# Split weights at sixteen different distances modulo 256 bytes from the activations, in a two-layer decoder kernel

## The chip, the cores and the metric

One core of a Trainium2 chip. The time is the device time of one execution in microseconds (us). Three runs of the kernel before gave a median of 1256.75 us (1255.97 to 1258.51).

## What is computed

Two layers over 256 positions of 1024 channels in float32: `x += 0.5*post1(SwiGLU_1(pre1(x)))`, then `x += postm(MIX(prem(x)))`, then a second SwiGLU step. MIX is one input projection that feeds three causal mixers (A: gated MLP over chunks of 128, B: dilated attention, C: stick-breaking attention), a sigmoid-gated merge and an output projection.

```
h = rms_norm(x, ffn1_pre_g[l])
x = x + 0.5 * rms_norm(swiglu(h, ffn1_wi[l], ffn1_wo[l]), ffn1_post_g[l])
h = rms_norm(x, mix_pre_g[l])
y = hybrid_mixer(h, w_in[l], ...)          # branches A, B, C, gates, w_o
x = x + rms_norm(y, mix_post_g[l])
h = rms_norm(x, ffn2_pre_g[l])
x = x + 0.5 * rms_norm(swiglu(h, ffn2_wi[l], ffn2_wo[l]), ffn2_post_g[l])
```

In branch C the scores get a strictly causal mask (0 or -1e30) before the log-space sums.

## The kernel before

**Weights.** All weights come as 1 MB units of 128 x 2048 float32, by SyncE's DMA queue, into two `raw` buffers (or, for some units of the FFNs that are combined by addition, into other tiles). The coroutine `splitter` (line 213) cuts each half unit into a high and a low part in the type fp32r: ScalarE writes `hi` (line 231), VectorE writes `lo = raw - hi` (line 232). Both go into a ring of eight buffers each, `hi` and `lo`, 128 x 1024 elements or 4096 bytes a partition (lines 228 and 229; the few units in `place` go to other tiles of the same size). A ring buffer comes free when the last matmul on it has been issued (`release`, line 266).

**Matmuls.** Activations are split in the same way into `hT`, `gT`, `yT` and `sA` tiles. `mm3` (line 391) adds three products: activation high times weight high (line 392), activation high times weight low (393), activation low times weight high (394). So of each three matmuls two stream a `hi` buffer and one a `lo` buffer; the 128 x 128 activation block is the stationary operand (a weight load, PEld, of its own before each matmul), the split weights are the moving operand, 512 columns at a time (256 in line 715). In `qk` (lines 670 to 699) the roles are exchanged: ring buffers are stationary, `hT` moves.

**Addresses.** The pools lie one behind another, `cp` (constants, `x`, `hT`), `rp` (`raw`, `hi`, `lo`) and `sp` (all else); within a pool tiles follow in the order in which their tags are first used, each in slots of a multiple of 32 bytes. After the 4-byte tile `mh` (line 273) every tile of `cp` and `rp` is a multiple of 256 bytes long, and in `sp` the small statistics tiles fill eight slots of 32 bytes. So `hT`, `raw`, all `hi` and `lo`, `gT`, `yT` and `sA` start at the same address modulo 256. Slices taken of them start at multiples of 512 bytes. Only `ident`, ahead of `mh`, starts 32 bytes lower modulo 256; it is the moving operand of the transposes (line 339), whose stationary operand is a tile of `sp`. In line 650 (branch A's gating, plain float32, two passes a matmul) `ws` is stationary and `v` moves: both at the common address modulo 256.

**Masks.** `load_consts` (line 298) runs once, in the first FFN. It loads two parts of the constants into tiles of the tag `w3` (four buffers, which also serve the FFN's `sg` and `cc` tiles) and casts them with VectorE into `mB` (bf16) and `uo`; the third part goes by DMA straight into `mC` (float32), which line 821 adds to branch C's scores, 16 times.

**Order.** A planner of estimated costs (`Clock`, the numbers after `yield`) sets the order in which coroutines issue their instructions; each engine takes its own in that order.

Of the kernel before, what the change touches and what calls it, by code (L numbers as in the profile page):

```python
# [9 lines left out]
F32 = mybir.dt.float32  # L10
F32R = mybir.dt.float32r
BF16 = mybir.dt.bfloat16
# [3 lines left out]
P = 128  # L16
# [19 lines left out]
def f32(ap):  # L36
    return ap.bitcast(F32)
# [40 lines left out]
def trunk(ctx, tc, x, wpk, gains, lnp, wst, bst, consts, out, depth=DEPTH):  # L78
    nc = tc.nc
    V, S, G, T = nc.vector, nc.scalar, nc.gpsimd, nc.tensor  # L80
    ck = Clock()

    cp = ctx.enter_context(tc.tile_pool(name="cp", bufs=1))
    rp = ctx.enter_context(tc.tile_pool(name="rp", bufs=2))
# [7 lines left out]
    def nm(s):  # L92
        cnt[0] += 1
        return f"{s}_{cnt[0]}"
# [7 lines left out]
    def w3_tile(n):  # L102
        return sp.tile([P, 768], F32, tag="w3", name=nm(n), bufs=4)
# [3 lines left out]
    RING = 8  # L107
    raws, halves, place = {}, {}, {}
    st_ = {"dma": 0, "pos": 0, "ring": 0, "free": RING}
# [3 lines left out]
    def load(dst, src):  # L113

        i = nc.sync.dma_start(dst, src)
        if lastdma[0] is not None:
            tc.add_manual_dep(i.ins, lastdma[0].ins.name, NOSYNC, reason="load order")
        lastdma[0] = i
# [9 lines left out]
    for l in range(depth):  # L128
        for st0, qj in ((0, QUADS), (33, None), (73, QUADS)):
            b = UNITS * l + st0  # L130
# [77 lines left out]
    def ready(n, kind, k):  # L208
        if kind[0] == "T":
            raw[n] = k.b if kind == "T3" else k.ffn["a" if kind == "T1" else "f"]  # L210
        return n in raw

    def splitter():
        for n, (kind, k) in enumerate(plan):
            while not ready(n, kind, k):
                next(ld)
            halves[n] = []
            for q in range(2):
                gate = place.get(n)
                while st_["free"] <= 0 if gate is None else not gate.on:  # L220
                    yield 0.2
                    gate = place.get(n)
                if gate is not None:
                    h = sp.tile([P, 1024], F32R, tag="q4", name=f"hi{n}_{q}", bufs=9)
                    lo = sp.tile([P, 1024], F32R, tag="q4", name=f"lo{n}_{q}", bufs=9)
                else:
                    st_["free"] -= 1
                    h = rp.tile([P, 1024], F32R, tag="hi", name=f"hi{n}_{q}", bufs=RING)
                    lo = rp.tile([P, 1024], F32R, tag="lo", name=f"lo{n}_{q}", bufs=RING)
                r = raw[n][q]  # L230
                S.copy(h, r)  # L231
                V.tensor_sub(lo, r, f32(h))  # L232
                halves[n].append((h, lo))
                yield 1.2
            if kind == "B11":
                f = k.ffn
                if "f" not in f:
                    f["f"] = [sp.tile([P, 1024], F32, tag="xn", name=nm("wf"), bufs=2) for _ in WQ]
                for q, c in enumerate(WQ):
                    V.tensor_add(f["f"][q], f["a"][q], k.b[q])  # L240
                    nc.gpsimd.dma_start(f["a"][q], wpk[k.u12][:, c], accum_op=ALU.add)
                    yield 0.6
            elif kind == "B21":
                for q in range(2):
                    V.tensor_add(k.ffn["f"][q], k.ffn["f"][q], raw[n][q])
                    yield 0.6
            elif kind == "T1":
                k.t1 = True
            done.add(n)
            for _ in range(3):  # L250
                next(ld, None)
# [41 lines left out]
    mB = [mB_[:, 768:1152], mB_[:, 0:768]]  # L293
    uo = cp.tile([P, 256], F32R, tag="uo", name="uo")
    nU, nO = uo[:, 0:P], uo[:, P:256]
    mC = cp.tile([P, 384], F32, tag="mC", name="mC")

    def load_consts():
        a = w3_tile("cst")
        load(a, consts[:, 0:768])  # L300
        V.tensor_copy(mB_[:, 0:768], a)
        a = w3_tile("cst")
        load(a[:, 0:640], consts[:, 768:1408])
        V.tensor_copy(mB_[:, 768:1152], a[:, 0:384])
        V.tensor_copy(uo, a[:, 384:640])
        load(mC, consts[:, 1408:1792])

    hT = cp.tile([P, NT, KD, 2, P], F32R, tag="hT", name="hT")
    hh, hl = hT[:, :, :, 0, :], hT[:, :, :, 1, :]
# [124 lines left out]
    def ffn(gi, nxt, first):  # L434
# [149 lines left out]
        for j in range(2, NCH - 1):  # L584
            if j == 4:
                if first:
                    load_consts()
                gain(gi + 1)
                gain(gi + 2)
            if j // 2 * 2 in QUADS:  # L590
                if j % 2 == 0:
                    pair7(j, ss)
                continue
            uo = take(1)[0]
            wo(uo, j - 2, 0, False)
            wo(uo, j - 2, 1, True)
            us = take(2)
            wi(us, j, 0, False)
            wi(us, j, 1, True)
# [335 lines left out]


    ck.start(splitter(), 7.0)
    for tt in range(NT):
        hready[tt] = Flag()
# [5 lines left out]
    for l in range(depth):  # L945
        b = 6 * l
# [102 lines left out]
```

## Time and profile before

| | |
|---|---|
| median of the runs | 1256.75 us |
| profiled execution, time / span | 1256.99 / 1255.3 us |
| TensorE matmuls | 1237.2 us, 99% of the span |
| weight loads | 1013.0 us, beside the matmuls |
| VectorE / ScalarE | 958.0 us (76%) / 738.7 us (59%) |
| DMA | 259.38 MB, 207 GB/s |

The span runs from the first instruction to the last; 1.7 us lie around it. A busy TensorE is not TensorE at its peak: matmuls overlap and their ends are modelled, so the pace of matmuls is read from the distance between their starts. Line numbers are those of the kernel before.

### The profile page before, as it was taken

The page shows a single profiled execution, that of the slowest core. Times are in us where ns is not written, and L with a number is a line of the kernel's source. Part 1 is how long each engine was busy: PE and PEld are TensorE (multiplying, and loading weights), DVE is VectorE, ACT ScalarE, POOL GpSimd, SP SyncE. Part 2 cuts the span into 40 slices and gives each one's busy share as a digit, 9 for nine tenths or more (in the row PEclk, how much of TensorE's full clock was granted, in tenths as well). Part 3 has the DMA queues.
Part 4 walks back from the last instruction along what each step waited for, and adds up shares of the span by engine and source line. Part 5 has one row for each costly group of instructions (what it writes and reads, how often), then busy time and mean ns, then how long its engine had stood idle before and what let it go on. Part 6 is the DMA issues. An engine that isn't in the chain of part 4 may idle for free.

```text
span 1255.3 us, 15804 instructions
## 1 busy us (share of the span) xinstructions
PE 1237.2 (99%) x5964; PEld 1013.0 (81%) x5964; DVE 958.0 (76%) x1215; ACT 738.7 (59%) x1026; POOL 77.2 (6%) x129
## 2 busy tenths in 40 slices
PE   8999999999999999999999999999999999999997
PEld 6777888888778888888888888888877788788886
DVE  5789977746765878899768899866477668688983
ACT  5566655545666465666645676654466655556662
POOL 0001001000000010010011000010000000111000
PEclk8999999999999999999999999999999999999999
DMA  7899555554335557895668785645543355687851
GB/s 252 273 320 268 173 201 193 191 212 173 129 135 183 188 181 268 253 284 170 248 215 244 257 256 194 238 167 182 188 170 132 134 201 201 202 240 241 255 186 66
DMA packets 45293, 259.38 MB, mean 207 GB/s; under 512 B 5280, under 2 KB 5408, under 8 KB 21280
## 3 DMA queue, kind: packets, MB, share of 16 engines
q1 hardware_dynamic: 38304, 233.20, 51.4%
q0 software_dynamic: 6912, 25.17, 10.6%
q8 instruction: 47, 0.77, 0.2%
q14 instruction: 30, 0.25, 0.1%
HBM read 257.30 MB, written 1.05 MB: 206 GB/s over the span
## 4 chain that ended last, share of the span: by engine, by line
PE 83%; DVE 6%; DMA 5%; ACT 3%; issue 1%; POOL 1%; SPq 0%; DVEq 0%; POOLq 0%; ACTq 0%
PE mm L392 15%; PE mm L394 15%; PE mm L393 15%; PE qk L681 6%; PE acc L394 5%; PE acc L393 5%; PE acc L392 5%; DMA raw<-wpk 4%; DVE lo L232 4%; PE qk L685 3%; PE tr L339 2%; ACT hi L231 2%; PE pj L392 1%; PE pj L394 1%; PE pj L393 1%; PE wo L394 1%
## 5 line engine op out<-in xcount | busy, mean ns | idle before, releaser
L232 DVE TENSOR_TENSOR lo<-raw,hi 128x1024 fp32r<-128x1024 f32 x376 | 453.0, 1221 | 121.1 <-ACT hi L231 115.9
L231 ACT CAST hi<-raw 128x1024 fp32r<-128x1024 f32 x376 | 387.5, 1050 | 191.6 <-DMA raw<-wpk 73.9
L392 PE MATMUL mm<-hi,hT 128*128 128x512 f32 x784 | 314.4, 401 | 1.5 <-ACT hT L332 1.5
L394 PE MATMUL mm<-hi,hT 128*128 128x512 f32 x784 | 307.7, 392 | 0.2 <-DVE hT L333 0.2
L393 PE MATMUL mm<-lo,hT 128*128 128x512 f32 x784 | 307.2, 392 | 0.0
L392 PEld LDWEIGHTS mm<-hi,hT 128*128 128x128 f32 x784 | 148.0, 189 | 33.1 <-issue 2.7
L394 PEld LDWEIGHTS mm<-hi,hT 128*128 128x128 f32 x784 | 147.8, 188 | 32.6 <-DVE hT L333 0.9
L393 PEld LDWEIGHTS mm<-lo,hT 128*128 128x128 f32 x784 | 148.2, 189 | 28.0
L392 PE MATMUL acc<-hi,gT 128*128 128x512 f32 x352 | 139.4, 396 | 0.0
L393 PE MATMUL acc<-lo,gT 128*128 128x512 f32 x352 | 137.9, 392 | 0.0
L394 PE MATMUL acc<-hi,gT 128*128 128x512 f32 x352 | 137.8, 392 | 0.0
L681 PE MATMUL qk<-hT,hi 128*128 128x512 f32 x320 | 111.3, 399 | 0.0
L685 PE MATMUL qk<-hT,lo 128*128 128x256 f32 x320 | 83.4, 281 | 0.0
L392 PE MATMUL mm<-hi,sA 128*128 128x512 f32 x192 | 77.2, 402 | 0.6 <-DVE sg L479 0.6
L394 PEld LDWEIGHTS acc<-hi,gT 128*128 128x128 f32 x352 | 66.2, 188 | 13.9 <-DVE gT L333 0.3
L393 PEld LDWEIGHTS acc<-lo,gT 128*128 128x128 f32 x352 | 66.2, 188 | 13.0
L392 PEld LDWEIGHTS acc<-hi,gT 128*128 128x128 f32 x352 | 66.2, 188 | 12.8
L394 PE MATMUL mm<-hi,sA 128*128 128x512 f32 x192 | 75.2, 392 | 0.0
L393 PE MATMUL mm<-lo,sA 128*128 128x512 f32 x192 | 75.0, 390 | 0.0
L332 ACT CAST gT<-tr 128x256 fp32r<-128x256 f32 x88 | 32.5, 369 | 64.2 <-PE tr L339 63.8
L681 PEld LDWEIGHTS qk<-hT,hi 128*128 128x128 f32 x320 | 57.8, 189 | 10.5
L685 PEld LDWEIGHTS qk<-hT,lo 128*128 128x128 f32 x320 | 60.5, 189 | 3.6
(168 smaller groups left out, 1623.7 us busy)
## 6 DMA issues: line engine op xcount, KB each, us to landing
raw<-wpk SPq DMA_DIRECT2D x187, 1024.0 KB, 4.8
wb<-wpk SPq DMA_DIRECT2D x24, 512.0 KB, 6.9
wb<-wpk POOLq DMA_DIRECT2D x24, 512.0 KB, 8.6
wa<-wpk SPq DMA_DIRECT2D x24, 512.0 KB, 6.0
wa<-wpk POOLq DMA_DIRECT2D x24, 512.0 KB, 9.2
gain<-gains SPq DMA_DIRECT2D x12, 512.0 KB, 7.5
x<-x SPq DMA_DIRECT2D x2, 512.0 KB, 5.6
raw<-wpk SPq DMA_DIRECT2D x2, 512.0 KB, 6.3
```

What stands on the lines that cost most here:

```text
L231: S.copy(h, r)
L232: V.tensor_sub(lo, r, f32(h))
L332: lasthi[0] = S.copy(h_out, src)
L339: T.transpose(tr[:, k * P:(k + 1) * P], src[:, k * P:(k + 1) * P], ident)
L392: T.matmul(o, ah, bh, start=first, stop=False, skip_group_check=go_on)
L393: T.matmul(o, ah, bl, start=False, stop=False, skip_group_check=go_on)
L394: T.matmul(o, al, bh, start=False, stop=stop, skip_group_check=go_on)
L681: T.matmul(o, h, hT[:, :, k, :, :], start=k == 0, stop=k == KD - 1)
L685: T.matmul(o[:, :, 0, :], lo, hh[:, :, k, :], start=False, stop=False)
```

## The change

A new helper `ring_half` gives each of the 16 ring buffers a tag of its own and a length of 1032 elements (4128 bytes), of which 1024 are used from element `b` on. With 32 bytes more a buffer, the pool lays `hi0`, `lo0`, `hi1`, `lo1` and so on 32 bytes apart modulo 256; `b` adds up to 28 bytes. The starts of the used parts lie, modulo 256 bytes from the activations: `hi` 0 to 7 at 0, 64, 128, 192, 4, 72, 144, 216; `lo` 0 to 7 at 32, 100, 168, 236, 48, 116, 184, 252. The ring still has eight pairs and each buffer is used again after eight. `mC` becomes bf16 (768 bytes a partition less, against 512 more for the ring): its constants are loaded into a third `w3` tile, and VectorE casts them.

```
--- before.py
+++ after.py
@@ -210,6 +210,13 @@
             raw[n] = k.b if kind == "T3" else k.ffn["a" if kind == "T1" else "f"]
         return n in raw
 
+    def ring_half(kind, n, q):
+
+        i = st_["ring"] % RING
+        t = rp.tile([P, 1032], F32R, tag=f"{kind}{i}", name=f"{kind}{'ABCDEFGH'[i]}_{n}_{q}", bufs=1)
+        b = i if kind == "lo" else (0, 0, 0, 0, 1, 2, 4, 6)[i]
+        return t[:, b:b + 1024]
+
     def splitter():
         for n, (kind, k) in enumerate(plan):
             while not ready(n, kind, k):
@@ -225,8 +232,8 @@
                     lo = sp.tile([P, 1024], F32R, tag="q4", name=f"lo{n}_{q}", bufs=9)
                 else:
                     st_["free"] -= 1
-                    h = rp.tile([P, 1024], F32R, tag="hi", name=f"hi{n}_{q}", bufs=RING)
-                    lo = rp.tile([P, 1024], F32R, tag="lo", name=f"lo{n}_{q}", bufs=RING)
+                    h, lo = ring_half("hi", n, q), ring_half("lo", n, q)
+                    st_["ring"] += 1
                 r = raw[n][q]
                 S.copy(h, r)
                 V.tensor_sub(lo, r, f32(h))
@@ -293,7 +300,7 @@
     mB = [mB_[:, 768:1152], mB_[:, 0:768]]
     uo = cp.tile([P, 256], F32R, tag="uo", name="uo")
     nU, nO = uo[:, 0:P], uo[:, P:256]
-    mC = cp.tile([P, 384], F32, tag="mC", name="mC")
+    mC = cp.tile([P, 384], BF16, tag="mC", name="mC")
 
     def load_consts():
         a = w3_tile("cst")
@@ -303,7 +310,9 @@
         load(a[:, 0:640], consts[:, 768:1408])
         V.tensor_copy(mB_[:, 768:1152], a[:, 0:384])
         V.tensor_copy(uo, a[:, 384:640])
-        load(mC, consts[:, 1408:1792])
+        a = w3_tile("cst")
+        load(a[:, 0:384], consts[:, 1408:1792])
+        V.tensor_copy(mC, a[:, 0:384])
 
     hT = cp.tile([P, NT, KD, 2, P], F32R, tag="hT", name="hT")
     hh, hl = hT[:, :, :, 0, :], hT[:, :, :, 1, :]
```

## Rows read from the trace of the kernel before

**Rows 1.** The profile's page, part 1: busy time, share of the span, instructions.

```profile
PE 1237.2 (99%) x5964; PEld 1013.0 (81%) x5964; DVE 958.0 (76%) x1215; ACT 738.7 (59%) x1026; POOL 77.2 (6%) x129
```

**Rows 2.** The page, part 4: the chain that ended last, by engine.

```profile
PE 83%; DVE 6%; DMA 5%; ACT 3%; issue 1%; POOL 1%; SPq 0%; DVEq 0%; POOLq 0%; ACTq 0%
```

**Rows 3.** All waits of TensorE, longest first: who for whom, us in total, times, longest.

```profile
PE tr L339 <- DVE sg L452: 3.9, 5, 1.7
```

**Rows 4.** Groups by line and shape, TensorE: busy us, mean ns | idle before.

```profile
L392 PE MATMUL mm<-hi,hT 128*128 128x512 f32 x784 | 314.4, 401 | 1.5 <-ACT hT L332 1.5
...
L392 PE MATMUL wo<-hi,hT 128*128 128x512 f32 x64 | 25.5, 399 | 0.0
```

**Rows 5.** Timeline of TensorE, 512 columns: start us, us, engine, line, instruction.

```profile
600.01 0.39 PE L394 MATMUL mm<-hi,hT 128*128 128x512 f32 x1
...
604.77 0.39 PE L394 MATMUL mm<-hi,hT 128*128 128x512 f32 x1
```

**Rows 6.** Timeline of TensorE, 256 columns (line 715).

```profile
268.59 0.28 PE L393 MATMUL mmv<-lo,hT 128*128 128x256 f32 x1
...
270.39 0.28 PE L393 MATMUL mmv<-lo,hT 128*128 128x256 f32 x1
```

**Rows 7.** One line's instructions: duration ns min/median/max; weight loads of 64, 128, 128 columns.

```profile
L855 PEld LDWEIGHTS avC<-eC,vC x32: 137/137/138, 332.8 to 999.2; 128*64 128x64 f32 x32
L392 PEld LDWEIGHTS mm<-hi,hT x784: 186/188/334, 10.5 to 1239.2; 128*128 128x128 f32 x196
L650 PEld LDWEIGHTS sv<-v,ws x32: 187/192/193, 221.4 to 847.5; 128*128 128x128 f32 x32
```

**Rows 8.** The same view, the matmuls of lines 650 and 339.

```profile
L650 PE MATMUL sv<-v,ws x32: 270/275/276, 221.5 to 847.6; 128*128 128x128 f32 x32
L339 PE MATMUL tr<-ident,mg x32: 270/272/273, 426.7 to 1050.8; 128*128 128x128 f32 x32
```

**Rows 9.** Timeline of TensorE: eight matmuls of line 650, four transposes of line 339.

```profile
221.54 1.05 PE L650 MATMUL sv<-v,ws 128*128 128x128 f32 x8
...
426.67 0.60 PE L339 MATMUL tr<-ident,mg 128*128 128x128 f32 x4
```

**Rows 10.** Timeline of TensorE in `qk`: moving operand in two runs.

```profile
280.08 0.28 PE L685 MATMUL qk<-hT,lo 128*128 128x256 f32 x1
...
281.84 0.28 PE L685 MATMUL qk<-hT,lo 128*128 128x256 f32 x1
```

**Rows 11.** Timeline of TensorE in branch C: 256 columns in two runs.

```profile
328.12 0.28 PE L839 MATMUL cu<-sh,uo 128*128 128x256 f32 x1
...
328.48 0.29 PE L842 MATMUL cu<-sh,uo 128*128 128x256 f32 x1
```

**Rows 12.** Groups by line and shape, VectorE: two operands in SBUF.

```profile
L232 DVE TENSOR_TENSOR lo<-raw,hi 128x1024 fp32r<-128x1024 f32 x376 | 453.0, 1221 | 121.1 <-ACT hi L231 115.9
...
L491 DVE TENSOR_TENSOR sA<-hT 128x512 f32<-128x512 f32 x16 | 10.8, 684 | 0.0
```

**Rows 13.** The same view: branch C's mask, branch B's bf16 mask, the cast to bf16.

```profile
L821 DVE TENSOR_TENSOR zC<-z,mC 128x384 f32<-128x384 f32 x16 | 8.3, 553 | 4.6 <-PE z L814 4.6
...
L738 DVE CUSTOM_DVE_ANT_0 pB<-s0B,mB 128x384 f32<-128x384 f32 x8 | 4.4, 550 | 0.0
...
L304 DVE CAST mB<-cst 128x384 bf16<-128x384 f32 x1 | 0.4, 360 | 0.3 <-DMA cst<-consts 0.3
```

**Rows 14.** Timelines of SyncE, VectorE, TensorE around the constants, with `mC`'s landing time.

```profile
74.74 0.44 SPq L115 DMA_DIRECT2D mC<-consts  x1
...
DMA to landing us min/median/max: 9.4/9.4/9.4
...
83.90 0.29 DVE L305 CAST uo<-cst 128x256 fp32r<-128x256 f32 x1
...
91.18 0.50 PE L392 MATMUL mm<-hi,sA 128*128 128x512 f32 x1 [0.56 <-DVE sg L479]
```

More of the change, by code (lines that the diff above doesn't have):

```diff
@@ L211, in ready, with ring_half @@
         return n in raw
+    def ring_half(kind, n, q):
+        i = st_["ring"] % RING
+        t = rp.tile([P, 1032], F32R, tag=f"{kind}{i}", name=f"{kind}{'ABCDEFGH'[i]}_{n}_{q}", bufs=1)
+        b = i if kind == "lo" else (0, 0, 0, 0, 1, 2, 4, 6)[i]
+        return t[:, b:b + 1024]
     def splitter():
@@ L227, in splitter @@
                     st_["free"] -= 1
-                    h = rp.tile([P, 1024], F32R, tag="hi", name=f"hi{n}_{q}", bufs=RING)
-                    lo = rp.tile([P, 1024], F32R, tag="lo", name=f"lo{n}_{q}", bufs=RING)
+                    h, lo = ring_half("hi", n, q), ring_half("lo", n, q)
+                    st_["ring"] += 1
                 r = raw[n][q]
@@ L295, in trunk @@
     nU, nO = uo[:, 0:P], uo[:, P:256]
-    mC = cp.tile([P, 384], F32, tag="mC", name="mC")
+    mC = cp.tile([P, 384], BF16, tag="mC", name="mC")
     def load_consts():
@@ L305, in load_consts @@
         V.tensor_copy(uo, a[:, 384:640])
-        load(mC, consts[:, 1408:1792])
+        a = w3_tile("cst")
+        load(a[:, 0:384], consts[:, 1408:1792])
+        V.tensor_copy(mC, a[:, 0:384])
     hT = cp.tile([P, NT, KD, 2, P], F32R, tag="hT", name="hT")
```

## The prediction

> **What bounds the kernel.** I read the busy times of the page first: matmuls fill 99% of the span, VectorE 76%, ScalarE 59% [rows 1]. The chain of work that ended last agrees: 83% of it is TensorE [rows 2]. Then the waits of TensorE: the largest of all comes to 3.9 us in the whole run [rows 3]. So the time is the pace of matmuls, and the next thing to read is the distance between their starts.
>
> In the timeline, 21 steps of matmuls with 512 columns take 604.77 - 600.01 = 4.76 us, 226.7 ns each [rows 5]. Fifteen steps with 256 columns take 270.39 - 268.59 = 1.80 us, 120 ns each [rows 6]. The difference, 106.7 ns for 256 columns, is 0.417 ns a column; 512 columns are 213.3 ns. Each matmul, long or short, so pays 13.3 ns on top. As it doesn't grow with the columns, it belongs to the change of weights, one load for each matmul. The groups of 512 columns on lines 392 to 394 run from `hT` with 784 for each line to `wo` with 64 for each [rows 4]; with the three groups between them (352, 192 and 80 for each line) that is 3 x 1472 = 4416 matmuls, 4416 x 13.3 ns = 58.7 us. This is what the change can act on: its moving operands, and what is loaded while they stream, now start at the same address modulo 256.
>
> **Part 1: the distances.** The question is whether the 13.3 ns come from both reads meeting at equal addresses modulo 256. A weight load of 64 columns takes 137 ns, one of 128 columns 188 ns [rows 7]: 0.80 ns a column, about twice the time of a moving column (0.417). While a load reads its 512 bytes (128 x 0.80 = 102 ns), the moving side reads 102 / 0.417 = 245 columns, 980 bytes. The distance between the two reads doesn't stay at its start: it grows by some 470 bytes, nearly two turns of 256. Whatever the start, the reads pass each other about equally often. A start of 0 isn't a lasting state, and another start takes nothing away.
>
> There is also a place where both go at one pace. On line 650 a load takes 192 ns, like the slow ones [rows 7], and the matmul's 128 columns take (1050 - 275) / 7 = 110.7 ns [rows 8, 9], also about 0.83 ns a column; the distance 0 is held from end to end. If equal addresses cost, it would be here. It pays 110.7 - 106.7 = 4.0 ns above 256 times 0.417 ns. The transposes, at distance 32, take (600 - 272) / 3 = 109.3 ns [rows 8, 9], 2.6 ns above. So distance 0, held throughout, costs at most 4.0 ns, and 1.4 ns more than distance 32; the 13.3 ns appear where it isn't held. (These are float32 matmuls, not fp32r, so it is a neighbour and no proof.) I take the gain of the distances as zero, with 0 and 13.3 ns as the ends.
>
> The trace shows 13.3 ns with each load. [...]
>
> **Part 2: odd starts.** The new starts are 4 to 28 bytes off the 32-byte grid for `hi` 4 to 7 and for `lo` 1 to 7. Per turn of the ring a `hi` is used twice and a `lo` once: 4 x 2 + 7 = 15 of 24 uses, 15/24 x 4416 = 2760 matmuls. No moving operand of the trace starts so; it may break its rows once more than now. The nearest rows are moving operands in two runs. In branch C three steps of 256 columns in two runs take 328.48 - 328.12 = 0.36 us, 120 ns [rows 11]: no more than in one run. In `qk`, five pairs (512 and 256 columns, two runs each) take 281.84 - 280.08 = 1.76 us, 352 ns a pair [rows 10], against 226.7 + 120 = 346.7: 2.7 ns a matmul. Ends: 0 and 2760 x 2.7 ns = 7.4 us. I take 0, because branch C's matmuls stream split data past a constant block as `mm3` does, while `qk` has its roles exchanged. A gain below nothing is excluded by no row and stands with the first rival.
>
> On VectorE, the split of 1024 elements takes 1221 ns and an addition of 512 takes 684 ns [rows 12]: (1221 - 684) / 512 = 1.05 ns an element, and the constant part is 147 ns. I cost odd starts at nothing here. What covers it is VectorE's quarter of idle time; were 100 ns added to each of the 376 splits of [rows 12], it would be 38 us on an engine with 1255.3 - 958 = 297 us to spare, and only in the stretches where TensorE waits for a split would any of it show.
>
> **Part 3: the mask.** Removed: nothing. Added: one DMA target that is a `w3` tile, and one cast of 128 x 384 to bf16, 0.36 us [rows 13]. Branch C's addition reads bf16 in place of float32: 16 x 553 ns before, and branch B's operation of the same width with a bf16 mask takes 550 ns [rows 13], so no change. The cast waits for its DMA: issued at 74.74, landed 9.4 us later at 84.14; the cast before it in VectorE's order ends at 83.90 + 0.29 = 84.19 [rows 14], so the wait is near zero. Queued behind it on VectorE are the splits, and TensorE waited 0.56 us for VectorE at 91.18 [rows 14], so VectorE is last there and 0.4 us goes on the path (0 if a later DMA hides it, 0.8 if the landing slips). SyncE's queue has the gains and the next `raw` unit behind the third load; a `w3` buffer last used two tiles earlier is free by then, so I cost that at nothing. If it weren't, SyncE would hold those loads until the transposes of the FFN's last `sg` tile are done.
>
> **Sum.** Distances 0, odd starts 0, mask +0.4 us. The profiled execution took 1256.99 us for a span of 1255.3; its sum is 1257.4. The median of the runs lies 0.24 us under the profiled one: 1257.2 us.
>
> **Rivals.**
> 1. *The distance matters in full.* For: the 13.3 ns are the same in all places, and all of them have distance 0. Against: the drift of nearly two turns and line 650. Only `hi` 0 stays at 0, 2 uses of 24: 4416 x 22/24 = 4048 matmuls x 13.3 ns = 53.8 us, 1203 us. If only half the distances help, some 1230.
> 2. *It matters as on lines 650 and 339.* 1.4 to 4.0 ns a matmul, say 2.7: 4048 x 2.7 = 10.9 us, 1246 us.
> 3. *Odd starts cost (the other side).* The place is the moving read of the 2760 matmuls, the price up to 2.7 ns [rows 10]: up to 7.4 us, 1265 us; at 2 ns, 1263. It decides from 1 ns a matmul (2.8 us). For: no large operand now starts off the 32-byte grid. Against: branch C's two runs at no price. [...]
> 4. *Odd starts cost much*: the affected streams fall to half their pace, 213 ns more. With the five buffers that start at odd multiples of 4 bytes (`hi` 4, `lo` 1, 3, 5, 7; 6 uses of 24): 1104 x 213 ns = 235 us, 1492 us. Nothing in the trace speaks for it.
> 5. *The change doesn't do what it says*: should the pool lay out the tiles in another order, the starts are other ones, and with them the cases above; the distances of 0 and the 32-byte shifts keep it among them. It has no chance of its own.
>
> **How the numbers follow.** Forecast 0.49, rival 1 0.14, rival 2 0.14, rival 3 0.18, rival 4 0.05. What a measurement of this kernel can tell from no change is about 0.2%, 2.5 us, so the forecast counts as no change, rivals 1 and 2 as faster, 3 and 4 as slower: 0.28, 0.49, 0.23. The range reaches from rival 2 to rival 3, 1245 to 1265 us (0.81). The forecast's own range is 1255 to 1259.
>
> **What would show each step.** The distance between starts of 512-column matmuls: 226.7 ns for all 16 buffers if I am right; 213 to 224 for some or all by rivals 1 and 2; by rival 3, higher on the buffers with odd starts alone, and it would then sort by `b`. Line 650 and the transposes, whose operands don't move, must keep 110.7 and 109.3 ns. VectorE's split stays at 1221 ns, line 821 at 553 ns. A third cast of 0.36 us stands near 84 us, with TensorE's wait near 91 us longer by about as much. The prediction is wrong if the 13.3 ns change by more than 0.5 ns on the mean.

## The result, and the profile after

| | before | after |
|---|---|---|
| median of the runs | 1256.36 us | 1270.99 us |
| ratio, 95% interval | | 1.0111 [1.0092, 1.0131] |
| profiled execution, time / span | 1256.99 / 1255.3 us | 1268.84 / 1267.1 us |

The changed kernel is 1.1% slower, outside the predicted range (1245 to 1265 us). The medians are from runs taken side by side; 1256.36 us is the same kernel as the 1256.75 us above. The profiled execution of the changed kernel is the shortest of its four. TensorE's granted clock is 0.996 in both profiled executions.

The page of the changed kernel, part 1 (busy us, share of the span, instructions) and the first line of part 4 (the chain that ended last, by engine):

```profile
PE 1253.0 (99%) x5964; PEld 1015.6 (80%) x5964; DVE 960.9 (76%) x1216; ACT 738.5 (58%) x1026; POOL 77.5 (6%) x129
...
PE 95%; DVE 2%; DMA 1%; ACT 1%; POOL 0%; issue 0%; SPq 0%; DVEq 0%; POOLq 0%; ACTq 0%
```

Matmuls are busy for 15.8 us more than in [rows 1], with as many instructions; VectorE and ScalarE have changed by 2.9 and 0.2 us. On the chain TensorE's share rose from 83% [rows 2] to 95%: TensorE takes longer, and waits less for the others. So the pace of matmuls comes next. The timeline of TensorE (start us, us, engine, line, instruction) in a stretch of 48 steps of 512 columns which both kernels run through without a break; first the kernel before:

```profile
545.56 0.48 PE L392 MATMUL mm<-hi,sA 128*128 128x512 f32 x1
545.87 0.39 PE L393 MATMUL mm<-lo,sA 128*128 128x512 f32 x1
546.11 0.40 PE L394 MATMUL mm<-hi,sA 128*128 128x512 f32 x1
546.34 0.39 PE L392 MATMUL mm<-hi,sA 128*128 128x512 f32 x1
...
547.49 0.39 PE L394 MATMUL mm<-hi,sA 128*128 128x512 f32 x1
547.71 0.39 PE L392 MATMUL acc<-hi,gT 128*128 128x512 f32 x1
547.94 0.39 PE L393 MATMUL acc<-lo,gT 128*128 128x512 f32 x1
...
556.55 0.39 PE L392 MATMUL mm<-hi,sA 128*128 128x512 f32 x1
556.78 0.39 PE L393 MATMUL mm<-lo,sA 128*128 128x512 f32 x1
```

The kernel after, the same work (its lines 401 to 403 are lines 392 to 394 of before):

```profile
549.40 0.47 PE L401 MATMUL mm<-hiE,sA 128*128 128x512 f32 x1
549.71 0.39 PE L402 MATMUL mm<-loE,sA 128*128 128x512 f32 x1
549.94 0.40 PE L403 MATMUL mm<-hiE,sA 128*128 128x512 f32 x1
550.18 0.40 PE L401 MATMUL mm<-hiF,sA 128*128 128x512 f32 x1
...
551.11 0.40 PE L402 MATMUL mm<-loF,sA 128*128 128x512 f32 x1
...
560.63 0.40 PE L401 MATMUL mm<-hiC,sA 128*128 128x512 f32 x1
560.86 0.40 PE L402 MATMUL mm<-loC,sA 128*128 128x512 f32 x1
```

Before, the first seven steps take 547.49 - 545.87 = 1.62 us, 231 ns each, and the 40 steps from 547.71 take 9.07 us, 226.8 ns each, the pace of [rows 5]. After, the first six take (551.11 - 549.71) / 6 = 233 ns and the other 42 take (560.86 - 551.11) / 42 = 232.1 ns. The pace starts alike, and only the kernel before settles to a faster one. The starts of all matmuls in the two traces say the same. A step is the distance between the starts of two consecutive matmuls of 512 columns; those under 300 ns are grouped by their place in the run of steps since the last interruption (a transpose, another shape, a wait):

```
                           before          after
steps 1 to 9 of a run    230.0 (1216)   232.3 (1211)   mean ns (count)
all later steps          226.7 (2879)   232.3 (2892)
all                      227.7 (4095)   232.3 (4103)
```

Place by place, the first three steps of a run take 232.2, 233.1 and 231.1 ns before and 232.5, 232.0 and 232.6 after; before, the tenth is at 226.8.

4.6 ns by 4416 matmuls is 20.3 us. From the first matmul to the last the profiled execution grew by 11.8 us only: steps of 512-column matmuls up to 330 ns added 21.8, `qk` gave back 0.8, transposes and the rest made no difference together (+0.5 and -0.6), and 9.1 us came back from the gaps over 330 ns, in which TensorE waits (59 gaps with 32.5 us before, 46 with 23.4 after). Thirteen fewer gaps are thirteen more steps; at 0.23 us each that moves some 3 us from one sum into the other, so by this estimate the longer steps added about 19 us and the waiting fell by about 6. By the medians the time grew by 14.63 us. Two of the waits that are left, in the view of all waits of TensorE (us in total, times, longest); the second is the one of [rows 3], 3.9 us before:

```profile
PE tr L348 <- DVE xn L369: 3.1, 3, 2.4
...
PE tr L348 <- DVE sg L461: 0.8, 3, 0.3
```

The other things that the prediction named haven't moved. Groups of VectorE by line and shape (busy us, mean ns | idle before), the split and the mask's addition:

```profile
L239 DVE TENSOR_TENSOR loA<-raw,hiA 128x1024 fp32r<-128x1024 f32 x46 | 56.2, 1222 | 32.4 <-ACT hiA L238 32.1
...
L830 DVE TENSOR_TENSOR zC<-z,mC 128x384 f32<-128x384 f32 x16 | 8.3, 553 | 4.6 <-PE z L823 4.6
```

Timeline of VectorE at the new cast:

```profile
81.97 0.36 DVE L315 CAST mC<-cst 128x384 bf16<-128x384 f32 x1
```

Timeline of TensorE: its wait after the cast, eight matmuls of branch A's gating, four transposes:

```profile
89.32 0.50 PE L401 MATMUL mm<-hiG,sA 128*128 128x512 f32 x1 [0.59 <-DVE sg L488]
...
231.23 1.05 PE L659 MATMUL sv<-v,ws 128*128 128x128 f32 x8
...
235.63 0.60 PE L348 MATMUL tr<-ident,u 128*128 128x128 f32 x4
```

The split takes 1222 ns (1221 in [rows 12]), the addition 553 as in [rows 13], the eight gating matmuls 1.05 us and four transposes 0.60 us as in [rows 9].

### The profile page after: what moved, and what is told of

Read it like the earlier page. It is cut to its first block, busy times and chain, and to the rows that moved or that the text cites. A ratio compares the mean times of both kernels' runs of the same rounds, so it can differ in the third digit from the quotient of the medians.

```text
span 1267.1 us, 15806 instructions
## 1 busy us (share of the span) xinstructions
PE 1253.0 (99%) x5964; PEld 1015.6 (80%) x5964; DVE 960.9 (76%) x1216; ACT 738.5 (58%) x1026; POOL 77.5 (6%) x129
## 3 DMA queue, kind: packets, MB, share of 16 engines
HBM read 257.30 MB, written 1.05 MB: 204 GB/s over the span
## 4 chain that ended last, share of the span: by engine, by line
PE 95%; DVE 2%; DMA 1%; ACT 1%; POOL 0%; issue 0%; SPq 0%; DVEq 0%; POOLq 0%; ACTq 0%
PE mm L401 18%; PE mm L403 17%; PE mm L402 17%; PE acc L403 6%; PE acc L402 6%; PE acc L401 6%; PE qk L690 6%; PE qk L694 3%; PE tr L348 3%; PE pj L403 1%; PE pj L401 1%; PE pj L402 1%; PE wo L402 1%; PE wo L403 1%; PE wo L401 1%; DMA cst<-consts 1%
## 5 line engine op out<-in xcount | busy, mean ns | idle before, releaser
L239 DVE TENSOR_TENSOR loA<-raw,hiA 128x1024 fp32r<-128x1024 f32 x46 | 56.2, 1222 | 32.4 <-ACT hiA L238 32.1
L239 DVE TENSOR_TENSOR loE<-raw,hiE 128x1024 fp32r<-128x1024 f32 x45 | 55.0, 1222 | 32.8 <-ACT hiE L238 32.7
L238 ACT CAST hiA<-raw 128x1024 fp32r<-128x1024 f32 x46 | 48.3, 1049 | 41.2 <-DMA raw<-wpk 13.5
L239 DVE TENSOR_TENSOR loG<-raw,hiG 128x1024 fp32r<-128x1024 f32 x43 | 52.6, 1222 | 16.4 <-ACT hiG L238 16.2
L239 DVE TENSOR_TENSOR loC<-raw,hiC 128x1024 fp32r<-128x1024 f32 x43 | 52.6, 1222 | 12.2 <-ACT hiC L238 11.8
L239 DVE TENSOR_TENSOR loB<-raw,hiB 128x1024 fp32r<-128x1024 f32 x46 | 56.2, 1222 | 4.7 <-ACT hiB L238 4.6
L239 DVE TENSOR_TENSOR loF<-raw,hiF 128x1024 fp32r<-128x1024 f32 x45 | 55.0, 1223 | 5.6 <-ACT hiF L238 5.5
L239 DVE TENSOR_TENSOR loH<-raw,hiH 128x1024 fp32r<-128x1024 f32 x43 | 52.5, 1220 | 3.4 <-ACT hiH L238 3.1
L239 DVE TENSOR_TENSOR loD<-raw,hiD 128x1024 fp32r<-128x1024 f32 x43 | 52.5, 1220 | 3.1 <-ACT hiD L238 2.8
L238 ACT CAST hiB<-raw 128x1024 fp32r<-128x1024 f32 x46 | 48.2, 1047 | 5.5 <-PE mm L403 3.4
L331 POOL TENSOR_SCALAR rs<-ss 128x1 f32<-128x1 f32 x24 | 11.8, 491 | 488.7 <-ACT sq L381 453.6
```

## The experiments

All of them keep the mask's part of the change. The ring is laid out anew in each, so "distance" is always that of the ring's used part from `hT`, modulo 256 bytes, unless said otherwise. Means in ns are over steps as above whose moving operand is a ring buffer. (The units that the planner puts in other tiles stay at distance 0, so means over all steps lie up to 0.3 ns nearer to 227.7.)

### One part alone, and one distance for all

**e1_mask_only** has the ring of before.

> Only the second part of the change: the mask in bf16, the ring as before (all distances 0). Theory D (the distance between the moving split weights and the stationary activations costs, and 0 is the cheapest) and theory N (it costs that neighbouring moving operands start at different addresses) both expect the time of the kernel before, 1257 us with at most 0.8 us more, and 226.7 ns between matmuls of 512 columns. Were the mask the cause, this kernel would take about 1271 us.

Measured: 1255.66 us, ratio 1.0005 [0.9993, 1.0016]; 227.6 ns a step. The mask costs nothing that can be measured; the whole loss is the ring's.

**e2_uniform64** and **e3_uniform128** move the ring as a whole by 64 and by 128 bytes, so that all starts stay at line starts. A line is here, and in the texts below, 16 bytes, counted from the address at which the activations start in the kernel before; the name stands for an order that the traces show. In the trace after, the buffers 4 bytes into a line (at distances 4, 100 and 116) take 236.0, 234.8 and 237.2 ns a step, and those 12 bytes in (236 and 252) 228.5 and 231.9; e11 has the same order in both halves of its ring. The code, shortened (the two pads are made once):

```
+  rp.tile([P, 16], F32, tag="padA", ...)     # e3: [P, 32]
   h = rp.tile([P, 1024], F32R, tag="hi", ..., bufs=RING)
   lo = rp.tile([P, 1024], F32R, tag="lo", ..., bufs=RING)
+  rp.tile([P, 48], F32, tag="padB", ...)     # e3: [P, 32]
```

> Mask in bf16, and all 16 ring buffers together 64 bytes further: one distance of 64 for all, no two moving operands that differ modulo 256, all starts on the 32-byte grid. Theory D: slower than the mask alone; in the changed kernel the buffer at distance 64 took 229.7 ns on the mean against 227.7 ns at distance 0 in the kernel before, so 4400 x 2 to 3 ns, 9 to 13 us, 1266 to 1270 us. Theory N (neighbours that differ): 1257 us, 226.7 ns. Theory O (odd starts alone cost): 1257 us.

> As the run at 64, with one distance of 128 for all. Theory D: the buffer at distance 128 took 232.4 ns in the changed kernel, so 4400 x 4.7 ns, some 20 us, 1277 us. Theories N and O: 1257 us.

Measured: 1261.68 us, 1.0044 [1.0029, 1.0059], 229.2 ns a step; and 1271.75 us, 1.0122 [1.0106, 1.0138], 232.5 ns. With 128 bytes alone, no odd start anywhere, the ring costs as much as the whole change. So neighbours that differ (theory N) and odd starts (theory O) are out as the only cause. Theory D's times, 1266 to 1270 and 1277 us, came out 4 to 8 and 5 us too long: at 64 its price was 1.5 ns, not 2 to 3, and it took nothing off for waits. The timeline of TensorE with 21 steps at 64 bytes:

```profile
124.14 0.40 PE L400 MATMUL mm<-lo,sA 128*128 128x512 f32 x1
...
128.95 0.39 PE L400 MATMUL acc<-lo,gT 128*128 128x512 f32 x1
```

The same view with 21 steps at 128:

```profile
46.54 0.39 PE L400 MATMUL mm<-lo,hT 128*128 128x512 f32 x1
...
51.42 0.39 PE L400 MATMUL mm<-lo,hT 128*128 128x512 f32 x1
```

(128.95 - 124.14) / 21 = 229.0 ns and (51.42 - 46.54) / 21 = 232.4 ns, in long runs without a break: neither settles to 226.7.

**e4_all_64** moves everything by 64 bytes, activations and ring, with one pad tile ahead of `x`: the distance is 0 again, the addresses are others.

> Mask in bf16, and everything behind the small tile mh (x, masks, activations, ring and all other tiles) 64 bytes further: the absolute address modulo 256 is that of the uniform-64 kernel's ring, the distance between weights and activations stays 0. Theories D, N and O: 1257 us. Theory A (the absolute start of the moving operand counts): as slow as the uniform-64 kernel.

Measured: 1257.55 us, 1.0007 [0.9998, 1.0017], 227.7 ns. So with all starts at line starts, what counts is the distance between two operands, not the address of one.

### Distance and line start told apart

From here the ring is cut from one long tile (or a tile for each pair), so that any start can be set (the code is shortened, the long tile is made once):

```
+  st_["rg"] = rp.tile([P, 2 * RING * 1024 + 64], F32R, tag="rg", ...)
+  c = st_["ring"] % RING * 1024 + d // 4
-  h = rp.tile([P, 1024], F32R, tag="hi", ...)
-  lo = rp.tile([P, 1024], F32R, tag="lo", ...)
+  h, lo = st_["rg"][:, c:c + 1024], st_["rg"][:, c + 8192:c + 9216]
```

**e5_one_tile_0** is the control, d = 0.

> Control for the next three: mask in bf16, the 16 ring buffers as slices of one long tile so that any distance can be set, here 0 for all. Every theory: the time of the mask alone, 1256 us, and 226.7 ns; if not, the form of the ring costs by itself.

Measured: 1256.2 us, 0.9998 [0.9987, 1.0008], 227.6 ns. The long tile itself changes nothing. By its 64 elements more, `gT`, `yT` and `sA` lie another 256 bytes from the ring, and their steps stay at 227.7, 227.1 and 227.9 ns (227.6, 227.1 and 227.9 in e1): a move of 256 costs nothing, one of 128 does. That is what the runs show for "modulo 256".

**e6_ring4_hT4** moves the ring and `hT` by 4 bytes (`hT` as elements 1 to 4096 of a tile of 4160); `gT`, `yT` and `sA` stay. Matmuls on `hT` are at distance 0 with odd starts, the others at distance 4.

> The ring and hT both 4 bytes further; gT, yT and sA stay. Theory D: matmuls on hT have distance 0 again and take 226.7 to 228 ns on the mean although every start is odd; those on gT and sA have distance 4 and take about 236 ns, as the buffer at distance 4 did in the changed kernel. In time: the 3 x (352 + 192 + 80) matmuls on gT, sA and yT pay 8 ns, 15 us, 1271 us. Theory O (odd starts cost by themselves): all groups are slow alike, 4400 x 8 ns, 1291 us.

Measured: 1291.43 us, 1.0285 [1.0267, 1.0304]. The timeline of TensorE, 21 steps on `hT`, then 21 on `gT`:

```profile
42.83 0.40 PE L398 MATMUL mm<-rg,hT 128*128 128x512 f32 x1
...
47.82 0.40 PE L398 MATMUL mm<-rg,hT 128*128 128x512 f32 x1
...
527.55 0.40 PE L398 MATMUL acc<-rg,gT 128*128 128x512 f32 x1
...
532.53 0.40 PE L398 MATMUL acc<-rg,gT 128*128 128x512 f32 x1
```

(47.82 - 42.83) / 21 = 237.6 ns on `hT` at distance 0, and (532.53 - 527.55) / 21 = 237.1 ns on `gT` at distance 4; over the whole trace 237.7 and 237.8. Were the distance all, the `hT` group would have kept 227.6 ns, so that theory fell: a moving operand that starts 4 bytes into a line of 16 costs about 10 ns (237.7 against 227.6), at distance 0 as at 4 (237.8), and on `gT` the stationary block isn't odd. The reverse (`hT` odd, the moving operand in one of the placed tiles at a line start, distance 252) takes 232.3 ns in 161 steps.

**e7_one_tile_236** and **e8_one_tile_192** are two distances that looked cheap and dear in the trace after (`lo` 3 and `hi` 3).

> One distance of 236 for all, an odd start. It was the cheapest of the nonzero distances in the changed kernel, 228.5 ns on the mean. Theory D with a price for each distance that can be carried over: 228 to 229 ns, 1257 to 1262 us. If a distance below 0 is better than 0, as a weight load a little ahead of the stream might be, under 226 ns and under 1254 us. If the price hangs on the neighbours' distances too: anything to 236 ns, 1290 us.

> One distance of 192 for all, on the 32-byte grid. The buffer at 192 took 232.8 ns in the changed kernel: 4400 x 5 ns, 22 us, 1278 us by theory D. 1257 us if only odd starts cost.

Measured: 1258.94 us, 1.0022 [1.0011, 1.0034], 228.8 ns; and 1272.6 us, 1.0136 [1.0118, 1.0153], 233.3 ns. 236 bytes, 12 bytes into a line, is the cheapest distance but 0 of those tried; 192 bytes, at a line start, is as dear as any line start tried for the whole ring.

### Many distances in one kernel

Three kernels, run once each, give each pair of the ring a tile and a start of its own, `hi` and `lo` of a pair at the same distance.

> Mask in bf16; each of the eight pairs of a hi and a lo buffer is one tile (rA to rH), pair number i at distance 32 x i, so eight distances on the 32-byte grid are read in one run, and within a half unit all moving operands have the same distance. Theory D (a price for each distance): rA (0) about 227.7 ns, rC (64) 229.2, rE (128) 232.5, rG (192) 233.3, as in the kernels with one distance for all; rB, rD, rF, rH (32, 96, 160, 224) not yet seen. In time some 1270 us. If a price exists only for the start within a line, all are 227.7 ns, which the run at 128 already speaks against.

> The same with 16 bytes more for each pair: distances 16, 48, 80 to 240, all at the start of a 16-byte line. Theory D: 228 to 236 ns; no distance below 226.7 ns, since the 13.3 ns of distance 0 are the floor of every kernel so far. A pair under 226 ns would make a kernel faster than both.

> The same with distances 36 x i: 0, 36, 72, 108, 144, 180, 216, 252, so the starts lie 0, 4, 8 or 12 bytes into a line of 16, twice each. If the place within the line has a price of its own (the ring and hT both 4 bytes further took 237.7 ns at distance 0), rB and rF (4 bytes in) are the slowest, 235 to 238 ns, rC and rG (8) 231 to 233, rD and rH (12) 228 to 232, as the changed kernel's buffers were. If only the distance counts, no order by 4, 8 and 12.

Measured: 1270.5, 1267.66 and 1273.07 us beside 1255.61 for the kernel before. Mean ns a step of each pair, over steps between two matmuls on the pair with a third on it just before:

```
e9_pairs_32    0: 231.4   32: 232.8   64: 229.5   96: 234.5  128: 232.5  160: 233.2  192: 232.7  224: 231.5
e10_pairs_16  16: 231.4   48: 231.5   80: 231.4  112: 230.6  144: 233.0  176: 231.7  208: 234.0  240: 232.6
e11_pairs_36   0: 228.9   36: 235.2   72: 234.2  108: 229.7  144: 231.2  180: 237.2  216: 235.3  252: 229.0
bytes into a line (e11)
               0           4           8          12           0           4           8          12
```

In e11 the place in the line orders the pairs, in both halves of the ring: 4 bytes in is dearest, 8 next, 12 on the mean no dearer than a line start. Its timeline of TensorE, six steps on the pair at 180 (`rF`), and five on the pair at 252 (`rH`):

```profile
552.89 0.39 PE L397 MATMUL mm<-rF,sA 128*128 128x512 f32 x1
553.12 0.40 PE L398 MATMUL mm<-rF,sA 128*128 128x512 f32 x1
...
554.32 0.40 PE L397 MATMUL acc<-rG,gT 128*128 128x512 f32 x1
...
558.49 0.39 PE L397 MATMUL acc<-rH,gT 128*128 128x512 f32 x1
558.72 0.39 PE L398 MATMUL acc<-rH,gT 128*128 128x512 f32 x1
...
559.63 0.39 PE L399 MATMUL acc<-rH,gT 128*128 128x512 f32 x1
```

(554.32 - 552.89) / 6 = 238 ns and (559.63 - 558.49) / 5 = 228 ns, on operands of one size a few us apart. At line starts, e9 and e10 find nothing under 229.5 ns, and the pair at distance 0 itself takes 231.4 in e9, not 227.6.

**e12_ring128_hT128** asks which operand is the partner. The ring and `hT` move by 128 bytes, so the ring is at distance 0 from `hT` and at 128 from `gT`, `sA` and `yT`, which stay.

> The ring and hT both 128 bytes further (everything at the start of a line); gT, sA and yT stay. Theory D: matmuls on hT are back at 227.7 ns on the mean, those on gT, sA and yT take 232.5 ns as with one distance of 128 for all. In time (352 + 192 + 80) x 3 x 4.9 ns, 9 us: 1265 us. If the partner of the distance is something else than the stationary activations (a write of the ring, the raw tiles, the absolute address), hT's matmuls stay at 232.5 ns, 1272 us.

Measured: 1265.51 us, 1.0076 [1.0053, 1.0099]. The timeline of TensorE on `hT`, then on `gT`:

```profile
47.44 0.39 PE L400 MATMUL mm<-rg,hT 128*128 128x512 f32 x1
...
52.20 0.39 PE L400 MATMUL mm<-rg,hT 128*128 128x512 f32 x1
...
520.31 0.39 PE L398 MATMUL acc<-rg,gT 128*128 128x512 f32 x1
...
525.19 0.39 PE L398 MATMUL acc<-rg,gT 128*128 128x512 f32 x1
```

(52.20 - 47.44) / 21 = 226.7 ns with `hT` stationary, (525.19 - 520.31) / 21 = 232.4 ns with `gT`. Over the whole trace it is 228.1 on `hT` against 232.4, 232.1 and 232.4 on `gT`, `sA` and `yT`. The same ring buffers are fast or slow by the activation block whose load goes with them. This shows the partner: the stationary operand.

### What is still dear alone, and what distance 0 needs

**e13_one_tile_112**, **e13_one_tile_252** and **e13_one_tile_32** put the whole ring at three of the distances met in mixed rings.

> One distance of 112 for all. As one of eight distances it took 230.6 ns on the mean, with 225 ns as its commonest value. Theory D with a fixed price for each distance: 230.6 ns, 1269 us. Theory P (the price is that of a pattern which a row of equal matmuls settles into): any value, and 225 ns for all and 1249 us if it settles on its commonest.

> One distance of 252, 4 bytes ahead of the activations, an odd start 12 bytes into a line. As one of eight: 229.0 ns; in the changed kernel 231.9 ns between matmuls at 216. Fixed price: 229 to 232 ns, 1262 to 1275 us. Theory P: any value from 226 to 232.

> One distance of 32. As one of eight 232.8 ns, in the changed kernel 233.9 ns. Fixed price: 233 ns, 1278 us. Theory P: any value from 226 to 236.

Measured: 1265.43 us, 1.0072 [1.0049, 1.0094], 230.8 ns; 1263.03 us, 1.0053 [1.0036, 1.0071], 230.3 ns; 1274.86 us, 1.015 [1.0126, 1.0173], 233.3 ns. Steps at 112 aren't equal, they go round in threes; the timeline of TensorE there:

```profile
577.36 0.39 PE L399 MATMUL mm<-rg,hT 128*128 128x512 f32 x1
577.58 0.39 PE L397 MATMUL mm<-rg,hT 128*128 128x512 f32 x1
577.81 0.40 PE L398 MATMUL mm<-rg,hT 128*128 128x512 f32 x1
578.05 0.39 PE L399 MATMUL mm<-rg,hT 128*128 128x512 f32 x1
```

577.36, 577.58, 577.81, 578.05: 220, 230 and 240 ns to the last printed digit; over the trace 225, 231 and 237 to 238 ns are the commonest values. A distance whose commonest step is 225 ns gives it back within three matmuls, so theory P's 225 ns for all didn't come; at all three distances the fixed price held, within 1.3 ns.

**e14_hi0_lo128** keeps every `hi` at distance 0 and puts every `lo` at 128 (`c + 8224` in place of `c + 8192`).

> All hi buffers at distance 0, all lo buffers at 128. Fixed price: hi matmuls (lines of the first and third product) 227.6 ns, lo 232.5 ns, mean 229.2, 1264 us. Theory P: the hi matmul that follows a lo one takes another time than the hi matmul that follows a hi one, and 227 ns is not seen in both.

Measured: 1266.68 us, 1.0084 [1.0059, 1.011]. The timeline of TensorE, 21 steps on `hT`:

```profile
45.46 0.39 PE L398 MATMUL mm<-rg,hT 128*128 128x512 f32 x1
...
50.31 0.39 PE L398 MATMUL mm<-rg,hT 128*128 128x512 f32 x1
```

(50.31 - 45.46) / 21 = 231.0 ns. If each matmul had the price of its own distance, it would be (2 x 227.6 + 232.5) / 3 = 229.2. The `hi` matmuls take 231.1 ns on `hT` and 231.6 on `gT` and `sA`, though their own distance is 0. By the place in a triple, over the whole trace: from a `hi` matmul to the `lo` behind it 232.5 ns, from `lo` to `hi` 232.4, from `hi` to the next `hi` 230.1. Even the last, with distance 0 at both its ends, isn't near 226.7; the matmul before it is a `lo`. So a step hangs on more than the two matmuls that it lies between. Steps grouped by place in a run (all steps of 512 columns) fit this:

```
mean ns           before   e5 (0)   e12   e14   e7 (236)   e3 (128)   e8 (192)   after
steps 1 to 9       230.0    229.9   231.3  231.8    229.0      232.0      233.2    232.3
later steps        226.7    226.7   229.8  231.4    228.7      232.3      233.0    232.3
```

Only where all neighbours are at distance 0 does the pace settle, within some nine matmuls, at 226.7 ns. (e12 is a mixture: it settles on `hT` alone.) Everywhere else it stays near its start.

No kernel was faster than the one before. So the loss of the change is in the main the loss of a settled state, which wants the same distance 0 for matmul after matmul. What happens between the two reads in that state, and what its 13.3 ns are, no run shows.

## Why the prediction was wrong

**What bounds the kernel**: right. The pace of matmuls is the time, and all of the loss is in it. One thing was left out: a slower TensorE waits less. Of the 20.3 us that 4.6 ns a matmul come to, 14.63 us show in the medians, so that some 6 us came back (in the profiled execution, the shortest of its four, 8), and the sums of the rivals had no such term.

**Part 1, the distances**: this step failed, in two places. The first is "A start of 0 isn't a lasting state, and another start takes nothing away." The count of meetings between the two reads was meant to show that the start doesn't matter. But distance 0 is, of all that were tried, the one start with a lasting state (226.7 ns after some nine matmuls), and every other start takes it away: 228.8 to 233.3 ns. The argument counted how often the reads pass each other within one matmul, while what counts reaches over more than one matmul (e14). The second is the ends. The trace held one distance only for the split weights, so its 13.3 ns could bound a gain, and no row bounded a loss. The prediction took 0 to 13.3 ns of gain; measured is a loss of 4.6 ns. A row that is seen at one setting bounds a gain at another at best, never a loss.

Line 650 was a poor neighbour: there distance 0 took 1.4 ns more than 32; with 512 columns of fp32r it takes 5.7 ns less (227.6 against 233.3), with 256 columns 3.1 more (119.8 against 116.7, e5 and e13_one_tile_32).

The same instructions take 227.6 ns a step at distance 0 (e1) and 233.3 at 32 or 192 bytes (e13_one_tile_32, e8), and e12 ties this to the block being loaded: 228.1 ns on `hT` at distance 0, 232.1 to 232.4 on the other three at 128.

**Part 2, odd starts**: the price was mis-sized, since branch C's two runs, which begin at line starts, stood in for starts inside a line; that such a start breaks an operand's rows once more was a guess, which no run shows. 4 bytes in costs 10 ns at distance 0 (e6), not 0 to 2.7. But in the change this is a small part. By the trace after, mean ns a step of each buffer, sorted by bytes into a line:

```
 0:  hiA 229.7  hiB 229.7  hiC 232.4  hiD 232.8  hiG 232.9  loA 233.9  loE 231.8
 4:  hiE 236.0  loB 234.8  loF 237.2
 8:  hiF 232.7  hiH 233.0  loC 231.9  loG 232.3
12:  loD 228.5  loH 231.9
```

Buffers at line starts are 2 to 6 ns above 227.7, `hi` 0 at distance 0 among them. e9, with line starts alone, takes 1270.5 us in its one run, against 1270.99. By uses (12, 4, 6 and 2 of 24) the four lines of the list come to 231.7, 236.0, 232.6 and 230.2 ns; with all uses at 231.7 the mean would be (4 x 4.3 + 6 x 0.9 - 2 x 1.5) / 24 = 0.8 ns lower. So by this estimate odd starts carry 0.8 ns of the loss, distance and mixing the other 4; that an odd buffer at a line start would take 231.7 was not run buffer by buffer. VectorE's part of this step was right, 1222 ns.

Of the three places inside a line, 12 bytes in is the cheapest (e11: 229.7 and 229.0 ns) and 4 bytes in the dearest (235.2 and 237.2).

**Part 3, the mask**: right. The cast takes 0.36 us at 81.97, TensorE's wait behind it is 0.59 us against 0.56 in [rows 14], and e1 bounds the whole at -0.07% to 0.16%.

**The rivals.** 1 and 2 (distance matters, as a gain) had the right cause with the wrong sign. 3 had the right side, and its time, 1265, missed by 6 us; its sign in the profile, higher on odd starts alone, isn't there, as line starts rose too. 4 is out: no buffer is near half pace. 5 is out: the buffers differ in the trace as their starts do.

## What to carry to other kernels

Where weights are loaded anew for each matmul, keep the moving operands of a long run at one distance from the stationary blocks, and try whole multiples of 256 bytes first: here, for 512 columns of fp32r, all other layouts tried were 0.2 to 2.9% slower. Don't start a moving operand 4 bytes past a multiple of 16 (10 ns a matmul at distance 0 here, 237.7 against 227.6). And where a trace shows one setting only, give the forecast an end on both sides, and take off what a slower bottleneck gives back in waits.

## What the runs showed of the hardware

- The best distance depended on the length here. Line 715's kind of matmul, 256 columns, takes 119.9 ns a step at distance 0 (as [rows 6]), but 113.4 at 192 and 113.3 at 112 (94 steps each; 116.7, 117.8 and 120.1 at 32, 64 and 128). In e8's timeline of TensorE:

```profile
271.86 0.28 PE L398 MATMUL mmv<-rg,hT 128*128 128x256 f32 x1
...
274.02 0.28 PE L399 MATMUL mmv<-rg,hT 128*128 128x256 f32 x1
```

(274.02 - 271.86) / 19 = 113.7 ns. So the prediction's reading of [rows 5] and [rows 6], 13.3 ns a matmul at either length, holds at distance 0 only; at 192, with the same 0.417 ns a column, it is 20.0 ns for 512 columns (233.3 - 213.3) and 6.7 for 256.
- In `qk`, with `hT` moving and the ring stationary, the 512-column step is 234.6 ns before, 231.7 after and 230.4 in e14 (`lo` alone moved), with the 256-column step at 117.1 to 117.6: there distance 0 isn't the best. With 308 such steps it is about 1 us, below what a measurement of this kernel can tell, and a ring with another distance for `qk` wasn't tried.
- Prices of a distance found in a mixed ring held within 1.3 ns when the whole ring got it: 229.5 and 229.2 at 64, 232.5 and 232.5 at 128, 230.6 and 230.8 at 112, 232.8 and 233.3 at 32, 232.7 and 233.3 at 192, 229.0 and 230.3 at 252. The exception is 0 (228.9 to 231.4 mixed, 227.6 alone).
